# Hybrid attention and gating block on one core: one pool of 8 KB tiles to the end, the queries' norm factor in the sigmoids, output weights split in the first projection, last product's operands formed sooner

## The chip, the cores and the metric

One core of one Trainium2 chip. The metric is the device time of one execution in microseconds (us); less is better.

## The reference, cut to what matters

2048 rows of width 1024, all float32. An input projection feeds 8 heads of stick-breaking attention and a gated unit; an output projection, a residual and a squared-ReLU MLP (1024 to 4096 to 1024) follow.

```python
h = rmsnorm(x, norm_mix_g)
q, k, v, u, vg = split(h @ w_in)
z = q @ k.T / sqrt(64)                       # causal, per head
A[t,s] = sigmoid(z_ts) * prod_{s<j<t} (1 - sigmoid(z_tj))
a_out = A @ v
b_out = gelu(u) * (W_s @ layernorm(gelu(vg)) + b)
mix = concat(rmsnorm(a_out, g_a), rmsnorm(b_out, g_b))
x = x + mix @ w_out
act = square(relu(rmsnorm(x, norm_mlp_g) @ w_up))
out = rmsnorm(x + act @ w_down, norm_final_g)
```

## The kernel before, in words

**Products.** Every float32 operand is split in two parts (`split`, L81 to L85): ScalarE (ACT) rounds it to the high part, VectorE (DVE) subtracts that from the source for the low part. `mm3` (L89 to L91) then multiplies in three passes. A form of a 128x512 operand thus costs one ACT and one DVE instruction, and TensorE (PE) waits for both.

**Stages.** Rows go in four chunks c of 512. `proj([0, 1])` runs alone from the start; `transposed_cols` makes keys and queries (columns times rows): its products leave PSUM by a DVE product with the row factors `r_row` (L181) and a split of that. From about 230 us `attention` is a generator that `together` steps beside the matrix products: `weigh` (z from `kt` and `qt`, a sigmoid of -z to `kk` at L351 and one of z to `b` at L353, a running product `pr` on DVE, L356 to L360), `turn` (transposes L370, split to `aT`), `gather`. Where an output projection `Out(c)` needs heads that aren't done, the attention is stepped alone (`while steps[0] < ...: next(side)`). `Out.operands` loads the gated half from `b_d` (L473), the attention from `a_d`, and weights: for c = 0 `weights` reads `w_out` (L512), splits it with `outg_t` (L84, L85) and stores the parts to `wo_d` (L544); later chunks load those (L509).

**MLP.** Chunks 0 and 1: `up_plain`, `down_plain`. Chunks 2 and 3: seven products in place of eight (`up_seven` over 16 q, `down_seven` over 4 groups g, the order of products in `ORDER` and `ORDER_D`). `Rights` holds the seven right operands of `up_seven` as split pairs `hc` of 8 KB tiles; the first is formed ahead, the other six by `rest` at q = 0. `Lefts` and `operand` form the left ones per q. `keep_acts` (L582 to L586) forms three sums of the activations on DVE and stores all seven pieces to `s_d`; it stands at the end of each q, on DVE with the next operands behind it. `Down.load(0)` (L807) loads the first weights of the last product, called before the last evacuation of q = 15; `down_seven` then forms left operands (`raw` from `s_d`) and right ones (`right`, with three GpSimd (POOL) differences per half h, L846 to L848).

**Pools.** Up to the end of `down_plain` 8 KB tiles `t8` come from the pool `mp`. Then `mp` is closed and a pool `mlp` opened over the same memory, so a tile of `mlp` waits for everything that still reads what lay there, the stores of `down_plain`'s results to `out_y` among it. In the part quoted, `together(down)` finishes the plain product first:

```python
    rights = Rights(rm)
    ahead = Lefts(rm, 0)
    together(down)
    low.close()
    ...
        loads = Down(rm)
        together(up_seven(rights, rm, ahead, lambda: loads.load(0)))
```

The order of an engine's instructions is otherwise set by a scheduler that goes by the order of the code and the free buffers. SyncE (SP) issues most DMAs, in its own order.

Of the kernel before, what the change touches and what calls it, by code (L numbers as in the profile page):

```python
# [8 lines left out]
F32 = mybir.dt.float32  # L9
F32R = mybir.dt.float32r  # L10
# [24 lines left out]
def block_kernel(ctx: ExitStack, tc: tile.TileContext, x, x_t, gmix, w_in, ln_g, ln_b, sgw, sgb,  # L35
# [24 lines left out]


# [47 lines left out]
    def proj(cs, places, sp, gated_first, staging):  # L109
# [4 lines left out]
        def stage(shape):  # L114
            return staging[0].tile([P] + shape, F32, name=staging[1], bufs=staging[2])
# [29 lines left out]
        def norms(c, pl):  # L145
            for tb in range(NTB):
# [7 lines left out]
                r = sp.tile([P, 1], F32, name="x_r", bufs=3 * NTB)  # L154
                nc.gpsimd.tensor_tensor(r, m, mhalf[:, 0:1], ALU.pow)
                rs.append(r)
# [139 lines left out]
        yield from transposed_cols(1, k_d)  # L296
        yield from transposed_cols(0, q_d)
# [18 lines left out]
    def attention(cs):  # L316
# [4 lines left out]
        def weigh(u, tb):  # L321
# [25 lines left out]
            if diag:  # L347
                nc.tensor.matmul(z[:, L - P:L], ident_b, neg_b, start=False, stop=True)
            kk = kks[kk_n[0] % NKK]
# [112 lines left out]
    class Out:  # L462
# [40 lines left out]
        def weights(self, half, part):  # L503

            rm = self.rm
            w = rm.pair([4, 512])
            if self.c > 0:
                for i in range(2):
                    nc.sync.dma_start(w[i].bitcast(F32), wo_d[half, part, i])  # L509
                return w  # L510
            st = rm.t8([4, 512])
            nc.sync.dma_start(st, w_out[part * 512:(part + 1) * 512, half * 512:(half + 1) * 512]  # L512
                              .rearrange("(n p) d -> p n d", p=P))
            for n in range(4):
                split(w[0][:, n], w[1][:, n], st[:, n], outg_t[:, part * 4 + n:part * 4 + n + 1])
            return w

        def product(self):
# [9 lines left out]
            def group(half, part, m, rr):  # L528
# [13 lines left out]
                if c == 0:  # L542
                    for i in range(2):
                        nc.sync.dma_start(wo_d[half, part, i], ws[i].bitcast(F32))  # L544
# [34 lines left out]
    def keep_acts(q, acts):  # L579

        a11, a12, a21, a22, s1, s2, s4 = (acts[:, i] for i in (0, 1, 6, 3, 4, 5, 2))
# [33 lines left out]
    def down_plain(rm):  # L615
# [25 lines left out]
        for g in range(ND):  # L641
            lefts, rights = {}, {}
            for turn in range(4):
# [7 lines left out]
                if n not in rights:  # L651
                    rights[n] = right(n, g)
                a, b = lefts[c], rights[n]
# [21 lines left out]
    class Rights:  # L675
# [22 lines left out]
        def rest(self, step):  # L698
            if step == 0:
                self.keep(4, self.b11)  # L700
                self.keep(5, self.t2)
                self.keep(1, self.b21)
                self.minus(self.b21, self.b21, self.t2)
            elif step == 1:
                self.keep(6, self.b12)
            else:
                self.keep(3, self.b21)
                self.keep(2, self.b22)
# [21 lines left out]
    def up_seven(rights, rm, ahead, before_last):  # L730
        hc = rights.hc
        for q in range(16):
            l = ahead if q == 0 else Lefts(rm, q)
            s12, a11, a12, a21, a22, w0, w4 = l.s, l.a11, l.a12, l.a21, l.a22, l.w0, l.w4
            if q == 0:
                rights.rest(0)
# [13 lines left out]
            if q == 0:  # L750
                rights.rest(1)
# [3 lines left out]
            if q == 0:  # L755
                rights.rest(2)
            w2 = l.operand(a12)
            acts = rm.get("acts", [7, TC])
            c11, c21, c22, c12 = acts[:, 0, :], acts[:, 1, :], acts[:, 3, :], acts[:, 6, :]
            u2, u3 = rm.get("t2", [TC]), c22  # L760
# [29 lines left out]
            keep_acts(q, acts)  # L790
            yield

    class Down:


        def __init__(self, rm):
            self.rm = rm

        def load(self, g):

            self.bs = []
            for h in range(2):
# [7 lines left out]
                self.bs.append([v[0], v[2], v[1], v[3]])  # L810

    def down_seven(loads, rm):
# [19 lines left out]
        for g in range(NG):  # L832
            last_g = g == NG - 1
            if g > 0:
                loads.load(g)
            bs = loads.bs
            new = rm.get("acts", [2, 2, 512])

            def right(i, h):

                b11, b12, b21, b22 = bs[h]
                t2 = new[:, h]
                b = rm.w8([2, 2, 512])
                split(b[:, 0], b[:, 1], {0: b11, 5: t2, 1: b21, 6: b12, 4: b11, 3: b21, 2: b22}[i])
                if i == 0:
                    nc.gpsimd.tensor_tensor(b11, b12, b11, ALU.subtract)  # L846
                    nc.gpsimd.tensor_tensor(t2, b22, b11, ALU.subtract)
                    nc.gpsimd.tensor_tensor(b12, b22, b12, ALU.subtract)  # L848
                elif i == 1:
                    nc.gpsimd.tensor_tensor(b21, b21, t2, ALU.subtract)  # L850
                return b

            banks = {}
            for n, i in enumerate(ORDER_D):
                st = rm.raw8([4, TC])
                nc.sync.dma_start(st, s_d[g][i])
# [5 lines left out]
                tiles = []  # L862
# [192 lines left out]
```

## Time and profile before

| what | us |
|---|---|
| median of 3 runs (2518.34 to 2525.99) | 2518.61 |
| the profiled execution | 2518.97 |
| its span | 2517.2 |
| PE busy in the span | 2430.1 |
| DVE / ACT / POOL busy | 1694.0 / 1145.2 / 309.8 |

The span is the time from the first to the last instruction of the profiled execution; some 2 us lie around it. "Busy" counts matmuls by modelled ends, so a busy PE may run at half its clock: the granted clock is a column of its own (1.00 is 2.4 GHz, 0.5 is 1.2 GHz).

### The profile page before, as it was taken

What the parts mean: (1) busy time and instruction counts of PE and PEld (TensorE: products, weight loads), DVE (VectorE), ACT (ScalarE), POOL (GpSimd) and SP (SyncE); (2) the same over time, 40 slices, a digit from 0 to 9 for tenths busy, and PEclk for the clock granted to TensorE, in tenths of its full rate; (3) what the DMA queues carried; (4) which work ended last, traced back from release to release, by engine and by line L of the source; (5) the groups of instructions that cost most, each with busy time, mean ns of one, the idle gap of its engine ahead of it and who ended that gap; (6) DMA issues with size and microseconds to landing.
All of it is one profiled execution on the core that took longest, in us unless ns stands there. A gap on an engine that the chain in (4) does not pass through costs nothing.

```text
span 2517.2 us, 30341 instructions
## 1 busy us (share of the span) xinstructions
PE 2430.1 (97%) x11424; PEld 1991.5 (79%) x11424; DVE 1694.0 (67%) x2280; ACT 1145.2 (45%) x2004; POOL 309.8 (12%) x255
## 2 busy tenths in 40 slices
PE   8999999997899999999999899999989999999998
PEld 7887788876677888888877688888867888778886
DVE  4643678877767666666668878644667556677788
ACT  5422446445536555555555534322244444433333
POOL 1100011000000000000000000000113322314432
PEclk9999999997999999999989999999999999999999
DMA  9747977679544343433364533343523434753422
GB/s 378 265 141 240 333 260 243 214 211 330 173 164 150 121 126 120 123 115 117 126 255 162 181 130 117 112 182 134 216 85 137 156 141 153 281 218 120 167 101 101
DMA packets 158226, 446.59 MB, mean 177 GB/s; under 512 B 12544, under 2 KB 28928, under 8 KB 138624
## 3 DMA queue, kind: packets, MB, share of 16 engines
q1 hardware_dynamic: 149744, 417.39, 48.5%
q0 software_dynamic: 4032, 25.17, 2.4%
q10 hardware_dynamic: 4304, 2.10, 0.3%
q8 instruction: 90, 1.47, 0.2%
q14 instruction: 56, 0.46, 0.1%
HBM read 314.59 MB, written 130.02 MB: 177 GB/s over the span
## 4 chain that ended last, share of the span: by engine, by line
PE 86%; DVE 8%; issue 3%; DMA 3%; ACT 1%; POOL 0%; POOLq 0%; SPq 0%; DVEq 0%; ACTq 0%
PE mm L91 24%; PE mm L90 24%; PE mm L89 23%; PE tr L370 4%; PE av L389 2%; PE z L346 2%; PE av L388 2%; PE z L345 2%; DVE w L82 2%; DVE t L82 1%; DVE pr L359 1%; PE mm L498 1%; DVE aT L82 1%; PE mm L263 1%; DMA t<-b_d 1%
## 5 line engine op out<-in xcount | busy, mean ns | idle before, releaser
L89 PE MATMUL mm<-t,t 128*128 128x512 f32 x1280 | 503.5, 395 | 0.4 <-DVE t L82 0.4
L91 PE MATMUL mm<-t,t 128*128 128x512 f32 x1280 | 503.5, 393 | 0.0
L90 PE MATMUL mm<-t,t 128*128 128x512 f32 x1280 | 502.3, 393 | 0.0
L359 DVE TENSOR_TENSOR_SCAN pr<-kk,pr,zeros 128x513 f32<-128x513 f32 x192 | 246.3, 1284 | 119.5 <-ACT kk L351 119.0
L351 ACT ACTIVATE kk<-z 128x512 f32<-128x512 f32 (+2 forms) x320 | 172.3, 538 | 296.3 <-PE z L346 158.7
L89 PEld LDWEIGHTS mm<-t,t 128*128 128x128 f32 x1280 | 242.4, 189 | 51.2 <-DVE t L82 0.8
L91 PEld LDWEIGHTS mm<-t,t 128*128 128x128 f32 x1280 | 241.8, 189 | 52.0
L90 PEld LDWEIGHTS mm<-t,t 128*128 128x128 f32 x1280 | 242.1, 189 | 50.0
L81 ACT ACTIVATE aT<-tr 128x512 fp32r<-128x512 f32 (+1 forms) x320 | 173.7, 545 | 107.6 <-PE tr L370 105.9
L82 DVE TENSOR_TENSOR aT<-tr,aT 128x512 fp32r<-128x512 f32 (+1 forms) x320 | 191.1, 598 | 21.6 <-ACT aT L81 21.3
L370 PE MATMUL tr<-ident,b 128*128 128x128 f32 x1088 | 180.9, 279 | 21.9 <-DVE aT L82 17.8
L90 PE MATMUL mm<-w,w 128*128 128x512 f32 x448 | 176.4, 394 | 8.8 <-DVE w L82 8.6
L81 ACT ACTIVATE t<-t 128x1024 fp32r<-128x1024 f32 x104 | 104.7, 1060 | 172.7 <-DMA t<-in_w_down 110.8
L370 PEld LDWEIGHTS tr<-ident,b 128*128 128x128 f32 x1088 | 133.0, 143 | 58.4 <-DVE aT L82 26.6
L91 PE MATMUL mm<-w,w 128*128 128x512 f32 x448 | 175.6, 392 | 0.0
L353 ACT ACTIVATE b<-z 128x512 f32<-128x512 f32 (+2 forms) x320 | 172.1, 539 | 2.6 <-PE tr L370 2.6
L356 DVE TENSOR_TENSOR_SCAN pr<-kk,zeros 128x128 f32<-128x128 f32 (+3 forms) x128 | 104.5, 820 | 96.9 <-ACT kk L351 96.7
L81 ACT ACTIVATE w<-raw 128x512 fp32r<-128x512 f32 (+1 forms) x135 | 106.4, 801 | 132.3 <-PE mm L91 119.9
L91 PE MATMUL mm<-t,w 128*128 128x512 f32 x380 | 150.4, 396 | 2.8 <-DVE w L82 2.8
L82 DVE TENSOR_TENSOR w<-raw,w 128x512 fp32r<-128x512 f32 (+1 forms) x135 | 149.0, 1106 | 3.4 <-ACT w L81 2.9
L90 PE MATMUL mm<-t,w 128*128 128x512 f32 x380 | 149.1, 393 | 1.4 <-DVE t L82 1.4
L82 DVE TENSOR_TENSOR t<-t,t 128x1024 fp32r<-128x1024 f32 x104 | 123.6, 1225 | 39.1 <-ACT t L81 19.4
(214 smaller groups left out, 4765.5 us busy)
## 6 DMA issues: line engine op xcount, KB each, us to landing
w_in<-wi_d SPq DMA_DIRECT2D x40, 1024.0 KB, 8.4
kt<-k_d SPq DMA_DIRECT2D x160, 256.0 KB, 4.9
t<-in_w_down SPq DMA_DIRECT2D x28, 1024.0 KB, 5.1
s_d<-acts SPq DMA_DIRECT2D x16, 1792.0 KB, 6.2
raw<-s_d SPq DMA_DIRECT2D x28, 1024.0 KB, 4.8
t<-wo_d SPq DMA_DIRECT2D x24, 1024.0 KB, 6.9
wi_d<-w_in POOLq DMA_DIRECT2D x20, 1024.0 KB, 9.5
vt<-v_d SPq DMA_DIRECT2D x80, 256.0 KB, 2.7
```

The lines of the kernel that those rows point to most:

```text
L81: nc.scalar.activation(hi, src, AF.Copy)
L82: nc.vector.tensor_tensor(lo, src, hi.bitcast(F32), ALU.subtract)
L89: nc.tensor.matmul(ps, lh, rh, start=first, stop=False, skip_group_check=more)
L90: nc.tensor.matmul(ps, lh, rl, start=False, stop=False, skip_group_check=more)
L91: nc.tensor.matmul(ps, ll, rh, start=False, stop=last, skip_group_check=more)
L345: nc.tensor.matmul(z[:, :Z], ql, kt[:, 0, :Z], start=True, stop=False)
L346: nc.tensor.matmul(z[:, :Z], ql, kt[:, 1, :Z], start=False, stop=not diag)
L351: nc.scalar.activation(kk[:, :L], z[:, :L], AF.Sigmoid, scale=-QK_SCALE)
L353: nc.scalar.activation(b[:, :L], z[:, :L], AF.Sigmoid, scale=QK_SCALE)
L356: nc.vector.tensor_tensor_scan(pr[:, L - 1::-1], kk[:, L - 1::-1], zeros[:, :L], 1.0, ALU.mult, ALU.add)
L359: nc.vector.tensor_tensor_scan(pr[:, ::-1], kk[:, ::-1], zeros, carry[tb], ALU.mult, ALU.add)
L370: nc.tensor.transpose(tr[:, tb * P:(tb + 1) * P], bs[tb][:, j * P:(j + 1) * P], ident)
```

## The change

1. `mp` stays open to the end: `mlp` is gone, and with it the tiles `acts` and `t2`. The seven pieces of the activations lie in one 8 KB tile and two 4 KB ones, stored by three DMAs in place of one.
2. `Rights.rest` is a generator, stepped with the last two turns of `down_plain`.
3. `Down.first` loads and forms the operands of the last product's first step before the last evacuation of `up_seven`.
4. `w_out` is split in `proj([0, 1])` (`split_w_out`), stored to `wo_d` by POOL's queue; `Out.weights` only loads.
5. Queries are not multiplied by the row factor; the two sigmoids take it as a per-partition scale (`rq`), for which `norms` makes a negated copy on POOL.

```diff
@@ proj
+        def split_w_out():
+            for half in range(2):
+                for k in range(0, KD, 2):
+                    st, hi, lo = stage([2, 512]), stage([2, 512], F32R), stage([2, 512], F32R)
+                    nc.sync.dma_start(st, w_out[...])
+                    for n in range(2):
+                        split(hi[:, n], lo[:, n], st[:, n], outg_t[:, k + n:k + n + 1])
+                    for i, w in enumerate((hi, lo)):
+                        nc.gpsimd.dma_start(wo_d[half, k // 4, i, :, k % 4:k % 4 + 2, :], w.bitcast(F32))
+                    yield
...
+                nc.gpsimd.tensor_tensor(rq[:, 1, i:i + 1], r, mone, ALU.mult)
...
-                    t = sp.tile([P, TC], F32, name="gelu_t", bufs=3)
-                    nc.vector.tensor_tensor(t, ps, r_rows[ci], ALU.mult)
-                    split(st[:, 0, :], st[:, 1, :], t)
+                    if col == 0:
+                        split(st[:, 0, :], st[:, 1, :], ps, QK_SCALE)
...
+        if cs[0] == 0:
+            yield from split_w_out()
@@ attention
-            nc.scalar.activation(kk[:, :L], z[:, :L], AF.Sigmoid, scale=-QK_SCALE)
+            nc.scalar.activation(kk[:, :L], z[:, :L], AF.Sigmoid, scale=rq[:, 1, row:row + 1])
-            nc.scalar.activation(b[:, :L], z[:, :L], AF.Sigmoid, scale=QK_SCALE)
+            nc.scalar.activation(b[:, :L], z[:, :L], AF.Sigmoid, scale=rq[:, 0, row:row + 1])
@@ Out.product
-                if c == 0:
-                    for i in range(2):
-                        nc.sync.dma_start(wo_d[half, part, i], ws[i].bitcast(F32))
@@ keep_acts
-        nc.sync.dma_start(s_d[q // 4][:, :, q % 4, :].rearrange("i p t -> p i t"), acts)
+        nc.sync.dma_start(dst[0:4, :, q % 4, :].rearrange("i p t -> p i t"), acts)
+        nc.sync.dma_start(dst[4:6, :, q % 4, :].rearrange("i p t -> p i t"), s12)
+        nc.sync.dma_start(dst[6, :, q % 4, :], s4)
@@ Down
+        def first(self):
+            self.load(0)
+            self.made = self.make(0, ORDER_D[0])
@@ the end
-    together(down)
-    low.close()
+    while not placed:
+        next(down)
+    rest = rights.rest()
+    if together(down, rest, 0.5) is OPEN:
+        together(down)
+    for _ in rest:
+        pass
...
-        together(up_seven(rights, rm, ahead, lambda: loads.load(0)))
+        together(up_seven(rights, rm, ahead, loads.first))
```

The change has 35 lines more ahead of these functions, so its line numbers differ: L82, L663, L672, L692 and L582 to L585 of before are L86, L686, L695, L715 and L600 to L603 of the change.

**Order on DVE where `down_plain` ends.** The tiles `mm` are the plain product's banks, `t8` the kept right operands, `w8` their sources. Before:

```order
L663 TENSOR_TENSOR t8_12265<-mm_15921,t8_12265 128x512
L672 SCALAR_TENSOR_TENSOR t8_12265<-t8_12265,nf_r_15917,gfin_t_5092 128x1024
L73 TENSOR_SCALAR nf_m_15938<-nf_ssq_15936 128x1
L672 SCALAR_TENSOR_TENSOR t8_12265<-t8_12265,nf_r_15940,gfin_t_5092 128x1024
L82 TENSOR_TENSOR t8_15953<-w8_15032,t8_15952 128x1024 x2
L82 TENSOR_TENSOR t8_15959<-w8_15033,t8_15958 128x1024 x2
L82 TENSOR_TENSOR t8_15965<-w8_15035,t8_15964 128x1024 x2
L82 TENSOR_TENSOR w8_15973<-s12_15055,w8_15973 128x512
L692 TENSOR_TENSOR w8_15035<-w8_15035,w8_15033 128x1024
```

Now, the plain product's last evacuations (L686) and four of the six kept operands in turns:

```order
L86 TENSOR_TENSOR t8_15849<-w8_15044,t8_15848 128x1024
L686 TENSOR_TENSOR t8_12274<-mm_15807,t8_12274 128x512
...
L686 TENSOR_TENSOR t8_12276<-mm_15841,t8_12276 128x512
L86 TENSOR_TENSOR t8_15869<-w8_15046,t8_15868 128x1024 x2
L686 TENSOR_TENSOR t8_12276<-mm_15861,t8_12276 128x512
L715 TENSOR_TENSOR w8_15046<-w8_15046,w8_15044 128x1024
L86 TENSOR_TENSOR t8_15891<-w8_15045,t8_15890 128x1024 x2
L715 TENSOR_TENSOR w8_15046<-w8_15046,w8_15044 128x1024
L686 TENSOR_TENSOR t8_12274<-mm_15881,t8_12274 128x512
```

The kept operands stood behind the last result of the plain product; four of six now stand ahead of its last four evacuations.

**Order on DVE where `up_seven` ends.** `raw` is the left operand's source, `t` (or `acts`) the right one's. Before:

```order
L82 TENSOR_TENSOR w_18153<-t_18117,w_18153 128x1024
L82 TENSOR_TENSOR w_18159<-raw_18144,w_18159 128x1024
L782 TENSOR_TENSOR acts<-mm,t_18017 128x512
L82 TENSOR_TENSOR w_18162<-t_18121,w_18162 128x1024
L788 TENSOR_TENSOR acts<-mm,t_18017 128x512
L82 TENSOR_TENSOR w_18226<-raw_18220,w_18226 128x1024
L582 TENSOR_TENSOR acts<-acts 128x512
L583 TENSOR_TENSOR acts<-acts 128x512
L584 TENSOR_TENSOR acts<-acts 128x512
L585 TENSOR_TENSOR acts<-acts 128x512
L82 TENSOR_TENSOR w_18229<-acts,w_18229 128x1024
```

Now:

```order
L802 TENSOR_TENSOR t_18068<-mm,t_18069 128x512
L86 TENSOR_TENSOR w_18183<-t_18169,w_18183 128x1024
L808 TENSOR_TENSOR t_18068<-mm,t_18069 128x512
L86 TENSOR_TENSOR w_18189<-raw_18178,w_18189 128x1024
L600 TENSOR_TENSOR t_18201<-t_18068 128x512
L601 TENSOR_TENSOR t_18201<-t_18201,t_18068 128x512
L602 TENSOR_TENSOR t_18068<-t_18068 128x512
L603 TENSOR_TENSOR t_18069<-t_18068,t_18201 128x512
L86 TENSOR_TENSOR w_18192<-t_18173,w_18192 128x1024
L86 TENSOR_TENSOR w_18281<-raw_18279,w_18281 128x1024
```

The right operand of the second half of the first step (`w_18162` before, `w_18192` now) stood ahead of the four instructions of `keep_acts` and now stands behind them.

**Order on SP there and at the first output projection.** In the change, at the end of `up_seven`:

```order
L606 DMA s_d_103<-t_18035 128x2x512
L605 DMA s_d_103<-t_17931 128x4x512
L607 DMA s_d_103<-t_17932 128x512
L827 DMA t_18169<-in_w_down 128x4x512
L827 DMA t_18171<-in_w_down 128x4x512
```

The stores of q = 14 now go ahead of the first weights; before, three of the four weight loads went ahead of the one store. At `Out(0)`, before:

```order
L512 DMA t_5101<-in_w_out 128x4x512
L331 DMA vt<-v_d 128x512
L329 DMA kt<-k_d 64x2x512 x2
L334 DMA qt<-q_d 128x512
L331 DMA vt<-v_d 128x512
L473 DMA t_5111<-b_d 128x4x512
L475 DMA t_5113<-a_d 128x4x512
L400 DMA a_d<-ao 128x512
L544 DMA wo_d<-t_5099 128x2048
```

and now:

```order
L532 DMA t_5150<-wo_d 128x2048
L532 DMA t_5151<-wo_d 128x2048
L499 DMA t_5154<-b_d 128x4x512
L501 DMA t_5156<-a_d 128x4x512
L356 DMA vt<-v_d 128x512
L354 DMA kt<-k_d 64x2x512 x3
L359 DMA qt<-q_d 128x512
L356 DMA vt<-v_d 128x512
```

The load of the gated half from `b_d` stood behind the next heads' keys and queries and now stands ahead of them.

## Rows read from the trace of the kernel before

**Rows 1.** The page, part 1: busy time, share and instructions by engine.

```profile
PE 2430.1 (97%) x11424; PEld 1991.5 (79%) x11424; DVE 1694.0 (67%) x2280; ACT 1145.2 (45%) x2004; POOL 309.8 (12%) x255
```

**Rows 2.** Windows inside the two long stretches of attention beside matrix products.

```profile
core 0: us, PE busy (x) PEld busy (x) DVE busy (x) ACT busy (x) POOL busy (x), PEclk, DMA share, GB/s
270.00:540.00 270.00, 270.00 (x1399) 222.80 (x1399) 207.77 (x355) 137.90 (x298) 24.55 (x24) 1.00 0.78 257
800.00:1280.00 480.00, 480.00 (x2374) 395.67 (x2373) 308.37 (x396) 272.18 (x520) 9.95 (x13) 1.00 0.40 128
```

**Rows 3.** Windows (same columns) where PE stops, and one of the first projection.

```profile
63.00:126.00 63.00, 63.00 (x294) 52.54 (x294) 43.53 (x81) 29.00 (x44) 10.23 (x13) 1.00 0.70 264
...
550.00:580.00 30.00, 23.82 (x124) 17.61 (x123) 26.46 (x40) 18.97 (x41) 1.69 (x2) 0.99 0.70 186
580.00:610.00 30.00, 22.33 (x92) 18.31 (x93) 22.46 (x38) 21.44 (x42) 5.00 (x5) 0.61 0.92 332
...
1860.00:1900.00 40.00, 29.52 (x108) 22.48 (x107) 31.57 (x36) 22.78 (x33) 11.38 (x11) 0.87 0.28 105
2180.00:2215.00 35.00, 29.66 (x120) 23.90 (x119) 25.68 (x19) 14.43 (x18) 16.92 (x6) 0.90 1.00 388
2215.00:2240.00 25.00, 22.85 (x101) 18.61 (x100) 20.88 (x19) 8.21 (x9) 6.57 (x2) 1.00 0.33 126
```

**Rows 4.** Timeline of PE at the start of `up_seven`: start, duration, instruction, [idle before it].

```profile
1869.89 0.50 PE L89 MATMUL mm<-t,raw 128*128 128x512 f32 x1 [2.03 <-ACT t L81]
1874.56 0.79 PE L90 MATMUL mm<-t,raw 128*128 128x512 f32 x1 [4.17 <-DVE t L82]
...
1890.58 0.79 PE L91 MATMUL mm<-t,w 128*128 128x512 f32 x1 [2.48 <-DVE w L82]
```

**Rows 5.** Timeline of ACT there: splits of the kept operands.

```profile
1868.78 2.01 ACT L81 ACTIVATE t<-w 128x1024 fp32r<-128x1024 f32 x2 [1.68 <-DMA out_y<-t]
...
1873.24 3.90 ACT L81 ACTIVATE t<-w 128x1024 fp32r<-128x1024 f32 x4 [1.98 <-DMA out_y<-t]
```

**Rows 6.** Timeline of SP at the first output projection.

```profile
566.04 1.79 SPq L512 DMA_DIRECT2D t<-in_w_out  x1
...
575.33 0.43 SPq L473 DMA_DIRECT2D t<-b_d  x1
```

**Rows 7.** Timeline of ACT there.

```profile
579.00 2.56 ACT L84 ACTIVATE t<-t,outg_t 128x512 fp32r<-128x512 f32 x4 [2.75 <-DMA t<-in_w_out]
...
588.36 0.63 ACT L480 ACTIVATE t<-t 128x512 bf16<-128x512 f32 x1 [2.47 <-DMA t<-b_d]
```

**Rows 8.** Groups of DVE by line and form: total, mean ns, idle before.

```profile
L181 DVE TENSOR_TENSOR gelu_t<-mm,r_row 128x512 f32<-128x512 f32 x32 | 22.0, 689 | 49.4 <-PE mm L91 49.2
...
L85 DVE SCALAR_TENSOR_TENSOR t<-t,outg_t,t 128x512 fp32r<-128x512 f32 x16 | 11.0, 744 | 0.4 <-ACT t L84 0.4
```

**Rows 9.** Groups of ACT: the largest form of the sigmoid, and one with a per-partition scale.

```profile
L351 ACT ACTIVATE kk<-z 128x512 f32<-128x512 f32 x224 | 135.4, 605 | 192.3 <-PE z L346 158.7 <-PE z L348 30.7 <-DVE pr L359 2.0
...
L84 ACT ACTIVATE qkv_st<-mm,x_r 128x512 fp32r<-128x512 f32 x16 | 10.9, 685 | 23.0 <-PE mm L91 14.3 <-DMA v_d<-qkv_st 7.9 <-DMA q_d<-qkv_st 0.8
```

**Rows 10.** Timeline of PE where `down_seven` begins.

```profile
2188.69 0.39 PE L89 MATMUL mm<-w,w 128*128 128x512 f32 x1
...
2206.01 0.79 PE L90 MATMUL mm<-w,w 128*128 128x512 f32 x1 [5.34 <-DVE w L82]
```

**Rows 11.** Timeline of DVE there.

```profile
2174.93 0.69 DVE L582 TENSOR_TENSOR acts<-acts 128x512 f32<-128x512 f32 x1 [0.44 <-ACT acts L590]
...
2193.89 2.57 DVE L582 TENSOR_TENSOR acts<-acts 128x512 f32<-128x512 f32 x1 [0.23 <-ACT acts L590]
...
2204.74 1.21 DVE L82 TENSOR_TENSOR w<-acts,w 128x1024 fp32r<-128x1024 f32 x1
```

**Rows 12.** Timeline of POOL there.

```profile
2185.42 2.94 POOL L846 TENSOR_TENSOR t<-t,t 128x1024 f32<-128x1024 f32 x1 [21.22 <-DMA t<-in_w_down]
...
2195.88 2.86 POOL L846 TENSOR_TENSOR t<-t,t 128x1024 f32<-128x1024 f32 x1
```

**Rows 13.** DMA of 2176 to 2216 us: packets, bytes, mean rate.

```profile
DMA packets 5239, 15.04 MB, mean 376 GB/s; under 512 B 208, under 2 KB 208, under 8 KB 4470
```

More of the change, by code (lines that the diff above doesn't have):

```diff
@@ L59, in block_kernel @@
     sgb_t = const.tile([P, 8], F32, name="sgb_t")
+    rq = const.tile([P, 2, NC * NTB], F32, name="rq")
+    mone = const.tile([P, 1], F32, name="mone")
+    nc.gpsimd.memset(mone, -1.0)
     q_d = dram.tile([NH, 2, HD, T], F32, name="q_d")
@@ L503, in weights @@
         def weights(self, half, part):
-            rm = self.rm
-            w = rm.pair([4, 512])
-            if self.c > 0:
-                for i in range(2):
[L509 to L515, printed above, removed]
+            w = self.rm.pair([4, 512])
+            for i in range(2):
+                nc.sync.dma_start(w[i].bitcast(F32), wo_d[half, part, i])
             return w
@@ L576, in turn, with keep_acts @@
                     nc.sync.dma_start(h_d[self.c - 2][kk], self.hT[kk])
-    def keep_acts(q, acts):
-        a11, a12, a21, a22, s1, s2, s4 = (acts[:, i] for i in (0, 1, 6, 3, 4, 5, 2))
+    PLACE = (0, 1, 6, 3, 4, 5, 2)
+    def keep_acts(q, acts, s12, s4):
+        a11, a12, a21, a22 = (acts[:, i] for i in range(4))
+        s1, s2 = s12[:, 0], s12[:, 1]
         nc.vector.tensor_tensor(s1, a21, a22, ALU.add)
@@ L652, in down_plain @@
                     rights[n] = right(n, g)
+                if g == ND - 1 and turn == 2:
+                    placed.append(True)
                 a, b = lefts[c], rights[n]
@@ L696, in keep, with rest @@
             split4(t, src)
[L698 to L708, printed above, removed]
+        def rest(self):
+            self.keep(4, self.b11)
+            yield
+            self.keep(5, self.t2)
+            yield
+            self.keep(1, self.b21)
+            yield
+            self.minus(self.b21, self.b21, self.t2)
+            self.keep(6, self.b12)
+            yield
+            self.keep(3, self.b21)
+            yield
+            self.keep(2, self.b22)
     class Lefts:
@@ L754, in up_seven @@
             w3 = l.operand(a22)
-            if q == 0:
-                rights.rest(2)
             w2 = l.operand(a12)
-            acts = rm.get("acts", [7, TC])
-            c11, c21, c22, c12 = acts[:, 0, :], acts[:, 1, :], acts[:, 3, :], acts[:, 6, :]
-            u2, u3 = rm.get("t2", [TC]), c22
+            acts, both = rm.t8([4, TC]), rm.t4([2, TC])
+            c11, c21, c12, c22 = (acts[:, i, :] for i in range(4))
+            u2, u3 = both[:, 0, :], c22
             b1 = rm.ps()
@@ L789, in up_seven @@
             relu2(c12, c12)
-            keep_acts(q, acts)
+            keep_acts(q, acts, rm.t4([2, TC]), both[:, 1, :])
             yield
@@ L810, in load, with make, right @@
                 self.bs.append([v[0], v[2], v[1], v[3]])
+        def first(self):
+            self.load(0)
+            self.made = self.make(0, ORDER_D[0])
+        def make(self, g, i):
+            if self.made:
+                tiles, self.made = self.made, None
+                return tiles
+            rm = self.rm
+            if i == ORDER_D[0]:
+                if g > 0:
+                    self.load(g)
+                self.new = rm.t8([2, 2, 512])
+            st = rm.raw8([4, TC])
+            nc.sync.dma_start(st, s_d[g][PLACE[i]])
+            tiles = []
+            for h in range(2):
+                a = rm.w8([2, 2, TC])
+                split(a[:, 0], a[:, 1], st[:, 2 * h:2 * h + 2, :])
+                tiles.append((a, self.right(i, h)))
+            return tiles
+        def right(self, i, h):
+            b11, b12, b21, b22 = self.bs[h]
+            t2 = self.new[:, h]
+            b = self.rm.w8([2, 2, 512])
+            split(b[:, 0], b[:, 1], {0: b11, 5: t2, 1: b21, 6: b12, 4: b11, 3: b21, 2: b22}[i])
+            if i == 0:
+                nc.gpsimd.tensor_tensor(b11, b12, b11, ALU.subtract)
+                nc.gpsimd.tensor_tensor(t2, b22, b11, ALU.subtract)
+                nc.gpsimd.tensor_tensor(b12, b22, b12, ALU.subtract)
+            elif i == 1:
+                nc.gpsimd.tensor_tensor(b21, b21, t2, ALU.subtract)
+            return b
     def down_seven(loads, rm):
@@ L861, in down_seven @@
                 ps = banks[key]
-                tiles = []
-                for h in range(2):
-                    a = rm.w8([2, 2, TC])
-                    split(a[:, 0], a[:, 1], st[:, 2 * h:2 * h + 2, :])
-                    tiles.append((a, right(i, h)))
+                tiles = loads.make(g, i)
                 def passes(tb, k):
@@ L972, in block_kernel @@
         gfin_t = gains.tile([P, D], F32, name="gfin_t")
[L973 to L975 removed]
+        placed = []
+        mp = ctx.enter_context(tc.tile_pool(name="mp", bufs=1, reuse_waits="tile"))
+        rm = Room(mp, ps_mm, dict(t8=N8, t4=3))
+        gmlp_t = rm.t4([D])
         nc.sync.dma_start(gmlp_t, gmlp.broadcast_to([P, D]))
         nc.sync.dma_start(gfin_t, gfin.broadcast_to([P, D]))
[L978 removed]
         hTs = []
```

60 lines of the change are left out of this document (20 added, 40 removed).

## The prediction

> **What bounds the kernel now.** I read the page's busy times first: TensorE is busy for 2430.1 of 2517.2 us and the next engine, VectorE, for 1694.0 [rows 1]. So only two things can be won: time in which PE stands still, and time in which it runs at half clock after standing still. The windows tell where these are. In the long stretches PE is busy for the whole window at a granted clock of 1.00, with VectorE at 64% to 77% and ScalarE at 51% to 57% [rows 2]; removing work of those two engines there gives nothing. The idle time sits at seams between stages [rows 3], and the change touches three of them. Last I read the timelines of each seam for what PE waited for [rows 4 to 7, 10 to 12].
>
> A seam's loss is its idle PE time plus what the clock took: (1 - granted clock) x window, which is an upper end, since the clock is also low while PE stands still. Start of `up_seven`: 40 - 29.52 = 10.5 us idle and 0.13 x 40 = 5.2 us of clock, together 15.7. First output projection: 30 - 22.33 = 7.7 idle and up to 0.39 x 30 = 11.7 of clock after 580 us, and 6.2 idle before it; about 20 in all. Start of `down_seven`: 5.3 + 2.2 idle and 0.10 x 35 = 3.5 of clock, together 11.0. These three numbers are all that the parts below can win there.
>
> **Kept operands beside the plain product (part 2 of the change).** Now PE waits four times at the seam, first for ScalarE's splits and then for VectorE's [rows 4]. The splits begin late for a reason outside the engines: two groups of them wait for the landing of `out_y` stores [rows 5], since the new pool lies over the tiles that those stores read. Behind that come twelve splits one after another, at 1.0 us each on ScalarE (3.90 us for four [rows 5]). With one pool open to the end and the splits stepped with the last two turns, four of the six pairs stand ahead of the plain product's last evacuations, as the order on DVE shows. PE needs each product's operand only when the ones before it are through: a product is 48 passes, and in these rows a pass starts every 0.23 us, so a product is about 2.7 us; the two pairs still behind the seam come as the sixth and seventh of seven products, over 13 us after its start, and are six splits of about 1.1 us away. What can go wrong is ahead of the seam: splits between evacuations hold a PSUM bank by two splits and a subtraction, about 3.6 us against a product of 2.7 us, with three banks to go round. I leave 1.5 us of loss and take **-14**, with ends -9 (one bank wait of 3 us and the clock after it) and -15.5.
>
> **Output weights split in the first projection (part 4).** There the change adds 16 splits on each of ScalarE (2.56 us for four [rows 7]) and VectorE (744 ns [rows 8]), 10 and 12 us, and 12.6 MB of traffic. PE is busy for all of 63 us there, VectorE has 19.5 us free in that window and the DMA engines 30% of it [rows 3]: cost 0, ends -1 and +3 (the `w_in` loads of the query columns stand behind the new loads on SP, the `wi_d` stores behind the new ones on POOL's queue). If that cover went, the price would be the 12 us.
>
> What it takes away is at the first output projection. Attention is stepped alone there and VectorE is the limit: 26.5 and 22.5 of 30 us [rows 3]. Four splits stand in the middle of it, 2.56 us of ScalarE after 2.75 us idle for the weights' landing [rows 7], and 4 x 0.744 = 3.0 us of VectorE [rows 8]. Both go. The twelve others lie beside PE's work and give nothing. The order on SP moves too: the `b_d` load was issued 9 us after the weights, behind keys and queries of the next head [rows 6], and ScalarE and PE waited for it until 588.36 [rows 7]; now it stands ahead of these. It should land some 5 us sooner; the next head's keys and queries land later by the 2 MB and more that now go ahead, at 376 GB/s [rows 13] some 5 us. That head isn't the one drained, so I count 3.0 + 5 = **-8**; ends -2 (its late keys stop the attention instead) and -13 (two thirds of the 20).
>
> **Last product's first operands sooner (part 3).** PE goes straight from `up_seven` into the first step at 2188.69 and stops 12 us later for 5.34 us [rows 10]. Cause in the rows: the four instructions of `keep_acts` take 0.69 us each for q = 14 and 2.57 us and more for q = 15 [rows 11], from 2193.89 to 2204.74, while POOL works on its differences, 2.9 us each [rows 12]; each VectorE instruction ends about when a POOL one does. PE's next operand stands behind them. The change doesn't take this away: `keep_acts` stays on DVE, and the second half of the *first* step now stands behind it. Worse, the stores of q = 14, 1.84 MB, now go ahead of the first weights on SP: at 376 GB/s [rows 13] that is 4.9 us. POOL's first difference started when two weight tiles were there, at 2185.42 [rows 12]; now at 2190.3, and the first split of a tile, which lands 2.7 us sooner, ends about 2189.8: 1.1 us of idle PE. The half step then lasts 5.7 us to 2195.5. `keep_acts` meets three differences, 2190.3 to 2199, ends near 2200.2, and the waiting operand is ready at 2201.4: 5.9 us of idle, and 3.5 of clock as now. 1.1 + 5.9 + 3.5 = 10.5 against 11.0. I take **0**, ends -6 and +6 (the stores ending earlier or later, POOL meeting `keep_acts` or not).
>
> **Queries without the row factor (part 5).** Of the 32 products at L181, half go, 11.0 us of VectorE [rows 8], all in the projection where PE is the limit: 0. The 640 sigmoids get a per-partition scale. No row shows a sigmoid with one. The nearest is a 128x512 ScalarE copy out of PSUM with such a scale, 685 ns against 605 for the sigmoid [rows 9]: 80 ns each, 51 us of ScalarE in all. Ends: 0 and 80 ns. Where PE is busy throughout, ScalarE has 43% free and more [rows 2], so most of it is covered. It shows where attention runs alone and the chain sigmoid, running product, product sets the pace: about 100 sigmoids there x 80 ns = 8 us, some of it beside VectorE's own work: I take **+3**, ends 0 and +8.
>
> By "ScalarE: Activation LUTs", section "What ACT_TABLE_LOAD costs", of the Trainium skill each such operand adds about 93 ns; that would be an estimate of 60 us in place of 51, and speaks against this part.
>
> **Small things.** Sixteen POOL products of one column and 32 more store issues on SP have nobody waiting, except perhaps the first row factor at 239 us: 0, ends 0 and +2. Other seams (660 to 700, 1370 to 1410) may be reshuffled by the scheduler by a few us either way.
>
> **Sum.** -14 - 8 + 0 + 0 + 3 = -19, from the profiled execution's 2518.97: **2500 us**. That execution lies 0.4 us above the median, so nothing is to be corrected.
>
> **Rivals.**
> - *The sigmoids set the pace (slower).* If ScalarE with 80 ns more were the limit of a step of attention, all 51 us would come out: 2518.97 - 22 + 51 = 2548. It decides as soon as over 60% of the 51 is exposed (30 us, against 22 won and 7.6 of tolerance). Against it: PE busy for 100% of 750 us [rows 2]. For it: `kk` gates the running product. Chance 5%.
> - *The wait at the seam moves ahead of it.* Splits hold PSUM banks, or tiles still wait for `out_y`: of 14 us only 6 come, 2508. For it: three banks only, and the stores are as late as before [rows 5]. Chance 13%.
> - *The first output projection gains nothing*, since the next heads' keys are late: 2507 or 2508. Chance 14%.
> - *`down_seven` starts clean*: POOL's differences come after `keep_acts`, which take 0.69 us each again: 8 of the 11 us go, 2492. Chance 13%. For it: the differences start 4.9 us later than now. Against it: `keep_acts` starts later too, behind the same evacuation. The Trainium skill ("SBUF — State Buffer", section "Who interferes with whom") has VectorE with two SBUF inputs and GpSimd shut each other out for a whole instruction, whichever comes second; the 2.57 us in place of 0.69 agree, and by that rule one difference that runs into `keep_acts` is enough to hold all of it.
> - *The change doesn't do what it says*: the buffers of the one pool are handed out so that the kept operands wait as before, 2512 to 2516. Chance 5%.
>
> **How the numbers follow.** The forecast has the other 50%. The range takes in the clean start with the good ends of the other terms, 2488, and the seam or output rival with a bad end, 2513. One measurement of this kernel can tell 0.3%, 7.6 us, from no change: faster means below 2511. All of the forecast, nearly all of the clean start and most of the two middle rivals lie there: 0.86. Same 0.09, slower 0.05.
>
> **What would show it.** Start of `up_seven`: PE idle under 2 us and no half clock, or else waits on evacuations just ahead of it. First output projection: the wait for `b_d` gone or before 584, no L512. `down_seven`: a stop of about 6 us in the middle of the first step, in place of after it, with `keep_acts` still at 2.5 us and more. Sigmoids of 128x512 near 685 ns with PE still at 100% in the long windows. I am wrong if PE shows new idle time beside attention, or if the half clock stays at the seams.

## The result, and the profile after

The change takes 2499.6 us (median of 4 runs, 2497.61 to 2501.7) against 2519.45 before (median of 4, 2518.34 to 2525.99), a ratio of 0.9914 with a 95% interval of 0.9896 to 0.9931. The forecast was 2500. The profiled executions (2518.97 and 2500.81) are 18.2 us apart; the terms named below come to 21.2 us, and other stretches take 3.2 back. The sum was right, its terms not all: the two large gains came in the size that was forecast, the cost of the sigmoids did not show, and a gain of about 6 us and a loss of about 4 were not foreseen.

The windows of the changed kernel at the same seams (columns as in [rows 2]); `up_seven` begins 8 us and `down_seven` 18 us earlier than before:

```profile
226.00:260.00 34.00, 33.56 (x153) 27.01 (x152) 7.49 (x13) 8.64 (x17) 3.59 (x11) 1.00 0.98 300
550.00:580.00 30.00, 23.70 (x114) 17.70 (x113) 25.90 (x38) 18.96 (x39) 2.51 (x2) 0.89 0.76 254
580.00:610.00 30.00, 26.32 (x135) 22.02 (x134) 15.79 (x28) 14.02 (x28) 3.21 (x5) 0.89 1.04 345
1843.00:1883.00 40.00, 39.22 (x170) 31.47 (x169) 33.07 (x42) 22.74 (x37) 17.45 (x16) 1.00 0.41 145
2155.00:2190.00 35.00, 27.68 (x111) 21.45 (x110) 24.07 (x20) 11.45 (x16) 14.66 (x5) 0.90 1.03 361
2190.00:2215.00 25.00, 23.61 (x105) 19.25 (x104) 17.55 (x20) 10.06 (x10) 9.89 (x4) 1.00 0.39 156
```

The first of these windows before, which [rows 3] don't have:

```profile
226.00:260.00 34.00, 29.78 (x131) 23.38 (x130) 8.43 (x18) 9.94 (x21) 2.52 (x5) 0.95 0.83 259
```

PE was idle for 4.2 us there and is for 0.4 now. Against [rows 3]: the start of `up_seven` has 0.8 us of idle PE in place of 10.5, at full clock. After 580 us PE's clock is 0.89 in place of 0.61, and VectorE, which was the limit, has 15.8 us of work in place of 22.5. The start of `down_seven` is no better.

Windows cut the work at other places in each kernel. So I also took PE's records one by one: the time from a matmul to the next, less 0.227 us for a 128x512 pass (0.109 for 128x128 and so on), summed over the same stretch of PE's work. This is what PE loses there, to waits, clock and slow passes, in us (below zero where passes are quicker than 0.227 us), for the two kernels and five of the runs below:

| stretch of the work | before | change | undo_scale | undo_wout | late_splits | tied_keep_acts | tied_pad32 |
|---|---|---|---|---|---|---|---|
| first projection | 3.4 | 5.5 | 6.2 | 4.9 | 5.2 | 5.0 | 5.6 |
| next projection begins (225 to 260 us) | 6.8 | 1.1 | 8.6 | 0.4 | 1.2 | 0.4 | 0.6 |
| first output projection | 28.8 | 20.1 | 20.5 | 27.0 | 18.5 | 21.7 | 18.4 |
| start of `up_seven` | 15.8 | 1.5 | 0.5 | 1.5 | 9.9 | 1.5 | 1.2 |
| rest of `up_seven` | 2.4 | 6.0 | 6.0 | 6.0 | 5.9 | 6.0 | -0.4 |
| start of `down_seven` | 10.8 | 12.6 | 11.3 | 12.7 | 11.2 | 6.4 | 5.9 |
| whole program | 145.5 | 127.5 | 141.0 | 130.1 | 131.9 | 118.6 | 109.0 |

The other stretches differ by up to 4 us from run to run. So do some that stand here: at the first output projection late_splits, tied_keep_acts and tied_pad32 have the change's instructions in the change's order, and lose 18.4 to 21.7 us.

### The profile page after: what moved, and what is told of

Same layout as the page of the kernel before. It is cut to its first block, busy times and chain, and to the rows that moved or that the text cites. A ratio compares the mean times of both kernels' runs of the same rounds, so it can differ in the third digit from the quotient of the medians.

```text
span 2499.1 us, 30545 instructions
## 1 busy us (share of the span) xinstructions
PE 2427.0 (97%) x11424; PEld 1986.8 (79%) x11424; DVE 1686.5 (67%) x2264; ACT 1197.9 (48%) x2004; POOL 322.1 (13%) x288
## 4 chain that ended last, share of the span: by engine, by line
PE 83%; DVE 8%; DMA 4%; issue 3%; ACT 2%; POOL 0%; SPq 0%; DVEq 0%; POOLq 0%; ACTq 0%
PE mm L94 23%; PE mm L95 23%; PE mm L93 23%; PE tr L396 4%; PE av L414 2%; PE av L415 2%; PE z L370 2%; PE z L371 2%; DVE w L86 2%; DMA v_d<-qkv_st 1%; DVE pr L385 1%; DMA w_in<-wi_d 1%; PE mm L524 1%; DVE t L86 1%; DVE aT L86 1%
## 5 line engine op out<-in xcount | busy, mean ns | idle before, releaser
L377 ACT ACTIVATE kk<-z,rq 128x512 f32<-128x512 f32 (+2 forms) x320 | 201.7, 631 | 289.0 <-PE z L371 177.0
L86 DVE TENSOR_TENSOR aT<-tr,aT 128x512 fp32r<-128x512 f32 (+1 forms) x320 | 190.7, 599 | 25.3 <-ACT aT L85 25.2
L379 ACT ACTIVATE b<-z,rq 128x512 f32<-128x512 f32 (+2 forms) x320 | 201.0, 629 | 2.8 <-PE tr L396 2.7
L86 DVE TENSOR_TENSOR w<-raw,w 128x512 fp32r<-128x512 f32 (+1 forms) x135 | 149.9, 1112 | 0.9 <-ACT w L85 0.4
L95 PE MATMUL mm<-t,w 128*128 128x512 f32 x380 | 150.3, 396 | 0.0
L93 PE MATMUL mm<-t,w 128*128 128x512 f32 x380 | 150.2, 395 | 0.0
L94 PE MATMUL mm<-t,w 128*128 128x512 f32 x380 | 150.2, 395 | 0.0
```

The costliest lines, as they stand in the source:

```text
L86: nc.vector.tensor_tensor(lo, src, hi.bitcast(F32), ALU.subtract)
L93: nc.tensor.matmul(ps, lh, rh, start=first, stop=False, skip_group_check=more)
L94: nc.tensor.matmul(ps, lh, rl, start=False, stop=False, skip_group_check=more)
L95: nc.tensor.matmul(ps, ll, rh, start=False, stop=last, skip_group_check=more)
L379: nc.scalar.activation(b[:, :L], z[:, :L], AF.Sigmoid, scale=rq[:, 0, row:row + 1])
```

## The experiments

Each run changes the changed kernel, which stands at 2499.6 us, in one thing unless it says otherwise.

**Part 2 undone.**

```diff
-    rest = rights.rest()
-    if together(down, rest, 0.5) is OPEN:
-        together(down)
+    together(down)
...
+            if q == 0:
+                for _ in range(3):
+                    next(rest)
```

with the rest of `rest` stepped further on in q = 0 of `up_seven`, as before.

> The change with part 2 undone: the six kept operands are formed at q = 0 of up_seven again, the pool stays open to the end. Theory: the 14 us of the seam came from the place of the splits in the order, so about 2512 to 2514 us, with some 10 us of idle PE and half clock at the start of up_seven as before. Rival: they came from the one pool (no wait for stores of out_y), then at most 2504 us and an idle of under 4 us.

Measured 2498.59 us (5 runs, 2498.06 to 2500.08), ratio 0.9925 (0.9912 to 0.9938). PE's timeline there has one wait, as in the change:

```profile
1855.13 0.50 PE L93 MATMUL mm<-x,raw 128*128 128x512 f32 x1 [0.78 <-DVE t L686]
```

The reason is in the order: on all five engines the instructions stand exactly as in the change. Once the tiles come from the open pool, the scheduler puts the splits ahead by itself; where the code calls them has no effect. So this was a repeat of the change. The rival is right that the pool did it, for with part 4 or part 5 undone the seam loses no more either (1.5 and 0.5 us in the table). The run says nothing yet on what the pool did: the earlier place, or no wait for `out_y`.

**The splits forced behind the last evacuation**, the pool left open and part 2 undone as in undo_rest; `tie` holds the five sources of the kept operands:

```diff
+                    if g == ND - 1 and turn == 3 and tb == NTB - 1:
+                        for src in tie:
+                            nc.vector.scalar_tensor_tensor(src[:, 0, 0:1], y[:, 0:1], 0.0, src[:, 0, 0:1], ALU.mult, ALU.add)
```

> The change with one pool as it is, but the six kept operands tied by five one-column VectorE instructions to the last evacuation of the plain product, so that they are split behind it as before, with no store of out_y in their way. Theory: the gain at the seam comes from their earlier place, so some 5 to 10 us come back (2504 to 2510 us) with over 3 us of idle PE and half clock at the start of up_seven. Rival: the waits for out_y made the loss, then at most 2502 us and under 2 us of idle.

Measured 2506.14 us (2505.45 to 2509.3), ratio 0.9957 (0.994 to 0.9973): 6.5 us came back. The window:

```profile
1843.00:1883.00 40.00, 34.89 (x133) 26.24 (x132) 34.09 (x44) 22.44 (x33) 14.28 (x12) 0.91 0.25 88
```

5.1 us idle and the clock at 0.91. In the table the seam loses 9.9 us, against 1.5 with the splits ahead and 15.8 before. So of the 14 us some 8 are the place. The other 6 are argued: before, ScalarE's splits waited 1.68 and 1.98 us for stores of `out_y` [rows 5], but VectorE's half of them also stood behind the last result, a little later than here, and no run separates the two.

**Part 3 undone.**

```diff
-        together(up_seven(rights, rm, ahead, loads.first))
+        together(up_seven(rights, rm, ahead, lambda: loads.load(0)))
```

> The change with part 3 undone: only the weights are loaded ahead, the first operands are formed in down_seven. Theory: part 3 is worth nothing, so 2498 to 2502 us, and the stop of about 6 us moves from the middle of the first step to behind it. Rival: forming the operands early is worth the first half of the step, then 2504 us or more.

Measured 2502.44 us (2501.3 to 2504.39), ratio 0.9941 (0.9927 to 0.9954). PE's waits there:

```profile
2170.31 1.20 PE L93 MATMUL mm<-w,w 128*128 128x512 f32 x4 [1.22 <-ACT w L85]
2183.39 0.79 PE L94 MATMUL mm<-w,w 128*128 128x512 f32 x1 [6.07 <-DVE w L86]
...
2203.69 0.75 PE L94 MATMUL mm<-w,w 128*128 128x512 f32 x1 [2.15 <-DVE w L86]
```

The stop did not move behind the first step; it is as in the change. Neither theory fits: the early call does not set the order in the first step. What it does comes later: here four evacuations stand ahead of VectorE's next splits where the change has them behind, and PE's third wait is 2.15 us, with 3.4 us at half clock after it that the change doesn't have. That is worth some 2 to 3 us (15.0 us lost at the start of `down_seven` in place of 12.6).

**Part 4 undone**, with `Out.weights` and its stores as before.

```diff
-        if cs[0] == 0:
-            yield from split_w_out()
...
+            for n in range(4):
+                split(w[0][:, n], w[1][:, n], st[:, n], outg_t[:, part * 4 + n:part * 4 + n + 1])
```

> The change with part 4 undone: the output weights are split in the first output projection again. Theory: 8 us come back there, 2507 to 2509 us, with the time lost between 550 and 620 us as before. Rival: the gain there came from the order of the loads or from part 5, then 2498 to 2502 us.

Measured 2504.88 us (2503.52 to 2509.82), ratio 0.9954 (0.994 to 0.9969): 5.3 us come back, and 6.9 in the table. The windows:

```profile
550.00:580.00 30.00, 20.51 (x104) 15.06 (x103) 26.79 (x40) 20.83 (x43) 1.78 (x2) 0.88 0.82 223
580.00:610.00 30.00, 25.75 (x112) 21.53 (x112) 23.07 (x39) 21.07 (x38) 4.23 (x5) 0.72 0.91 341
```

VectorE is at 26.8 and 23.1 of 30 us again, as in [rows 3]. The theory holds for the size, at somewhat less than its 8. PE's longest wait there is another than before, though, for keys and not for `b_d`:

```profile
576.95 0.55 PE L355 MATMUL z<-kt,qt 128*128 128x256 f32 x1 [4.39 <-DMA kt<-k_d]
```

The first square on `b_d` is at 582.77 us and waits 0.35 us for the load. So the run does not confirm the 5 us that the prediction gave to the order of the `b_d` load.

**Part 5 undone.**

```diff
-                        split(st[:, 0, :], st[:, 1, :], ps, QK_SCALE)
+                    nc.vector.tensor_tensor(t, ps, r_rows[ci], ALU.mult)
+                    split(st[:, 0, :], st[:, 1, :], t)
...
-AF.Sigmoid, scale=rq[:, 1, row:row + 1])
+AF.Sigmoid, scale=-QK_SCALE)
```

> The change with part 5 undone: queries are multiplied by the row factor again and the sigmoids take a constant scale. Theory: the scale costs about 3 us where attention runs alone and gains nothing elsewhere, so 2496 to 2498 us, sigmoids of 128x512 at 605 ns. Rival: the shorter path of the queries took away the waits at 230 to 260 us, some 5 us, then 2501 to 2503 us and those waits are back.

Measured 2511.33 us (12 runs, 2505.74 to 2514.45), ratio 0.9973 (0.9963 to 0.9982). I expected a small gain and lost 12 us. PE's timeline after 240 us has the old waits again, first before:

```profile
240.28 0.49 PE L162 MATMUL mm<-ident,x_r 128*128 128x128 f32 x2 [1.49 <-POOL x_r L155]
...
254.89 0.39 PE L345 MATMUL z<-kt,qt 128*128 128x256 f32 x1 [2.73 <-DMA qt<-q_d]
```

then this run:

```profile
243.03 0.49 PE L180 MATMUL mm<-ident,rq 128*128 128x128 f32 x2 [1.49 <-POOL rq L173]
...
259.30 0.55 PE L365 MATMUL z<-kt,qt 128*128 128x256 f32 x1 [3.49 <-DMA qt<-q_d]
```

The rival had the place right: 7.5 us of the loss are there. The rest lies for the most part in three later stretches of PE's work, which stood at 610 to 620, 660 to 700 and 1500 to 1700 us before: each loses some 3 us more than in the change. The next run loses about as much in them without the loss at 240 us, so that part belongs to something else.

**Only the scale made constant**, in both sigmoids.

```diff
-AF.Sigmoid, scale=rq[:, 1, row:row + 1])
+AF.Sigmoid, scale=-1.0)
...
```

> The change with constant scales in the 640 sigmoids and nothing else altered; the queries' row factor is left out of the computation. This measures the cost of the per-partition scale alone. Theory: 3 us, so 2496 to 2498 us, sigmoids of 128x512 at 605 in place of some 685 ns. Rival: covered everywhere, 2498.5 to 2501 us; or more exposed than I counted, 2494 us or less.

Measured 2503.0 us (2500.17 to 2504.13), ratio 0.9937 (0.9924 to 0.9951). ScalarE's groups, first the change:

```profile
L377 ACT ACTIVATE kk<-z,rq 128x512 f32<-128x512 f32 x224 | 155.7, 696 | 203.4 <-PE z L371 177.0 <-PE z L373 24.0 <-DVE pr L385 1.5
L379 ACT ACTIVATE b<-z,rq 128x512 f32<-128x512 f32 x224 | 155.4, 695 | 2.8 <-PE tr L396 2.7
```

then this run:

```profile
L379 ACT ACTIVATE b<-z 128x512 f32<-128x512 f32 x224 | 135.6, 606 | 2.5 <-PE tr L396 2.5
L377 ACT ACTIVATE kk<-z 128x512 f32<-128x512 f32 x224 | 135.5, 605 | 180.3 <-PE z L371 152.7 <-PE z L373 25.3 <-DVE pr L385 1.3
```

Each of these sigmoids is 90 ns shorter, 448 of them 40 us, and the program isn't faster. But it is not a pure test: without `rq` as an operand the scheduler puts several hundred of PE's instructions elsewhere between 260 and 1500 us, and the order on VectorE and ScalarE changes too. Where the prediction put the cost, in PE's work that stood at 560 to 610 us before, this run loses 19.9 us and the change 19.4 by the count of the table. So no cost of the scale shows in these runs; that it is nothing is not shown.

**Part 5 undone as above, and the norms' squares out of the way.** The row norms write their squares to a scratch tile that only serves as a target; it is one of three `gelu_t` buffers, which the queries' products also take.

```diff
-                junk = sp.tile([P, D], BF16, name="gelu_t", bufs=3)
-                nc.scalar.activation(junk, xt, AF.Square, accum_out=ssq)
+                nc.scalar.activation(xt, xt, AF.Square, accum_out=ssq)
```

> Part 5 undone as in the run undo_scale, but the squares of the row norms are written over their source tile and no longer take one of the three gelu_t buffers, which the queries' products hold. Theory: what part 5 won at 230 to 260 us is the freed buffer, since the norms of the next chunk no longer wait for the queries' products; then the waits for row factors and queries there are gone (under 2 us lost in place of 8), and the time is 2498 to 2505 us against 2511 of undo_scale. Rival: it is the shorter path from the products to the queries' store; then the waits stay and the time too.

Measured 2498.38 us (2496.68 to 2501.25), ratio 0.9924 (0.9911 to 0.9937): as quick as the change, with all 16 products back. The window of 226 to 262 us, first of undo_scale:

```profile
226.00:262.00 36.00, 30.37 (x133) 23.94 (x131) 6.65 (x14) 7.90 (x17) 2.52 (x5) 0.95 0.77 228
```

and of this run:

```profile
226.00:262.00 36.00, 36.00 (x165) 29.45 (x163) 11.23 (x20) 8.21 (x17) 2.09 (x7) 1.00 0.97 309
```

PE has no idle time left. The first square of the next chunk starts at 222.40 us here, at 223.26 in the change and at 237.30 in undo_scale:

```profile
222.40 1.06 ACT L167 ACTIVATE st<-st 128x1024 f32<-128x1024 f32 x1 [2.00 <-DMA st<-in_x]
```

```profile
237.30 1.04 ACT L168 ACTIVATE gelu_t<-st 128x1024 bf16<-128x1024 f32 x1
```

So the gain of part 5 was neither VectorE's time nor the queries' path but a buffer.

**`keep_acts` of q = 15 later in the code**, behind the operands of the fourth step of `down_seven`.

```diff
+            if q == 15:
+                loads.late = lambda: keep_acts(...)
...
                 tiles = loads.make(g, i)
+                if g == 0 and n == 3:
+                    loads.late()
```

> The change with the four sums and three stores of keep_acts for q = 15 put behind the operands of the last product's fourth step. Theory: they, held by POOL's differences, make the stop of 6 us in the first step; without them ahead the stop and the half clock behind it go, 7 to 9 us: 2491 to 2493 us. Rival: the operand waits for its weights or for POOL as well, then it moves by under 3 us.

Measured 2498.56 us (2497.4 to 2500.72), ratio 0.9924 (0.9911 to 0.9936). A miss: the scheduler put the four sums where they were, and the stop was 6.09 us. So it says nothing on the theory, and I tied them:

```diff
+                loads.late = lambda b: (
+                    nc.vector.scalar_tensor_tensor(acts[:, 3, 0:1], b[:, 0, 0, 0:1].bitcast(F32), 0.0,
+                                                   acts[:, 3, 0:1], ALU.mult, ALU.add),
+                    keep_acts(q, acts, rm.t4([2, TC]), both[:, 1, :]))
...
+                if g == 0 and n == 2:
+                    loads.late(tiles[1][1])
```

> As late_keep_acts, but a one-column VectorE instruction makes the first sum of keep_acts for q = 15 wait for the second operand of the third step, since the place in the code alone did not move it. Theory: the sums, stretched by POOL's differences, make the stop of 6 us; now the second half's operand needs only its weights and ScalarE's split, 4 to 8 us go: 2491 to 2495 us, a stop under 2.5 us in the first step. Rival: POOL's differences hold VectorE's splits just as long, so the stop stays within 2 us of what it was or turns up one step later, 2496 us or more.

Measured 2493.05 us (2492.02 to 2496.46), ratio 0.9904 (0.9891 to 0.9917), 6.5 us less. PE's waits in the first steps:

```profile
2175.89 0.50 PE L94 MATMUL mm<-w,w 128*128 128x512 f32 x1 [1.82 <-DVE w L86]
2182.57 0.50 PE L94 MATMUL mm<-w,w 128*128 128x512 f32 x1 [0.95 <-DVE w L86]
2189.44 0.50 PE L94 MATMUL mm<-w,w 128*128 128x512 f32 x1 [1.13 <-DVE w L86]
```

One stop of 6 us became three short ones, with the clock at full speed. VectorE's splits there now take the POOL differences' pace (3.29 us in place of 1.2), so the contention is not gone, only what stood in its queue.

**The tiles 12 KB lower in the pool.** While the changed kernel has no wait in `up_seven`, it makes fewer passes per 100 us than before. Windows of before and of the change:

```profile
1905.00:2005.00 100.00, 100.00 (x438) 81.94 (x437) 62.92 (x88) 48.75 (x85) 30.50 (x22) 1.00 0.43 155
```

```profile
1890.00:1990.00 100.00, 100.00 (x432) 80.75 (x431) 60.77 (x81) 48.59 (x84) 29.75 (x22) 1.00 0.41 148
```

```diff
+        mp.tile([P, 4, 512], F32, name="t8", bufs=N8)
         gmlp_t = rm.t4([D])
```

> The change with the 8 KB tiles laid out at the start of the pool, ahead of the three 4 KB ones, 12 KB lower than in the change. In the change a pass of up_seven with a kept operand out of this pool takes 233.2 ns, before 229.2 ns; with the operand outside it 229 ns in both. Theory: the place of these tiles in memory makes the difference, so 229 to 230 ns again and some 4 us less, 2494 to 2496 us. Rival: it is what else goes on in up_seven (three stores, sums in the same pool), then 233 ns and 2498 to 2500 us.

Measured 2497.44 us (2495.72 to 2502.4), ratio 0.9921 (0.9908 to 0.9935), and the passes as slow as in the change (233.2 ns). The shift by 12 KB, a multiple of 512 bytes, is not it. But the two constants that part 5 adds also move all tiles of that side of SBUF, by 160 bytes (128 and 32). So two runs, on top of tied_keep_acts:

```diff
     mone = const.tile([P, 1], F32, name="mone")
+    const.tile([P, 8], F32, name="pad")
```

> The run tied_keep_acts with an unused constant of 32 bytes per partition behind mone. The change's two new constants moved every tile of the left side of SBUF up by 160 bytes: addresses that were 32 above a multiple of 64 bytes lie on one now, while the left operands of up_seven, on the right side, stay 32 above one. 32 bytes more bring both to the same remainder again. Theory: the remainder makes the slower passes, so 229 in place of 233 ns in up_seven and 3 to 5 us less than tied_keep_acts (2493.05): 2488 to 2490 us. Rival: addresses don't matter, 233 ns and 2492 to 2495 us.

Measured 2486.47 us (2482.18 to 2490.66), ratio 0.9883 (0.9866 to 0.9899).

> The same with 64 bytes: the left side's tiles lie on a multiple of 64 bytes (of 512 even) again, by another shift. Theory of the remainder: 233 ns as in the change and as in tied_keep_acts, 2492 to 2495 us. Rival, that any shift other than the change's is quick, or that 512 bytes are what counts: 229 ns or less and 2488 to 2490 us.

Measured 2493.89 us (2490.13 to 2495.23), ratio 0.9904 (0.989 to 0.9919). The windows in `up_seven`, first with 32 bytes:

```profile
1870.00:1970.00 100.00, 100.00 (x443) 82.81 (x442) 62.95 (x85) 49.65 (x87) 32.01 (x23) 1.00 0.42 148
```

then with 64:

```profile
1880.00:1980.00 100.00, 100.00 (x431) 80.50 (x430) 61.60 (x83) 48.85 (x85) 28.91 (x21) 1.00 0.41 151
```

443 passes against 431, with an unused 32 bytes, and 7.4 us between two programs whose instructions stand in one order. The theory of the remainder holds in its direction for these four layouts; with 32 bytes both the pass (226.7 ns) and the time are below what it gave. The run with 32 bytes is also the quickest version found: its median is 13 us below the change's, but the kernel before was also some 4 us quicker beside these two runs (2515.67 us), so against that the gain is about 9.

## Why the prediction was right, and where its steps were not

- **Start of `up_seven`, -14: right in size (15.8 to 1.5 us lost), wrong in cause.** The step "with one pool open to the end and the splits stepped with the last two turns" gave the stepping a share. It has none: undo_rest is the same program. The pool did all of it, some 8 us by the earlier place and the rest, as argued, by the waits for `out_y`. The bank waits that I left 1.5 us for came to one of 0.78 us. In the prediction "a product is 48 passes" is a slip: a product of `up_seven` has 12, and the 2.7 us that it goes on with is the time of 12.
- **First output projection, -8: right in size, its two parts not shown apart.** 28.8 to 20.1; undone alone it is 5 to 7 us. The wait for L512 is gone. The squares on `b_d` begin at 580.33 us in place of 588.36 [rows 7], of which some 2 us are the lead that the change has by 560 us; and undo_wout has the loss back with hardly a wait for `b_d`. What could be won there was more than the prediction's "about 20": its own three terms, 7.7, 11.7 and 6.2, make 25.6.
- **The new splits in the first projection, 0: right.** That stretch loses 5.5 us in place of 3.4, but 4.9 with part 4 undone, so at most about 0.6 us of it is theirs.
- **Start of `down_seven`, 0: nearly right, in its own steps.** PE's timeline in the change:

```profile
2171.08 1.21 PE L93 MATMUL mm<-w,w 128*128 128x512 f32 x4 [1.20 <-ACT w L85]
2184.16 0.80 PE L94 MATMUL mm<-w,w 128*128 128x512 f32 x1 [6.08 <-DVE w L86]
```

  1.1 and 5.9 us were forecast. VectorE shows `keep_acts` again at POOL's pace, as in [rows 11]:

```profile
2174.38 2.45 DVE L600 TENSOR_TENSOR t<-t 128x512 f32<-128x512 f32 x1 [0.37 <-ACT t L611]
2176.86 2.75 DVE L601 TENSOR_TENSOR t<-t,t 128x512 f32<-128x512 f32 x1
2179.54 2.83 DVE L602 TENSOR_TENSOR t<-t 128x512 f32<-128x512 f32 x1
2182.30 0.68 DVE L603 TENSOR_TENSOR t<-t,t 128x512 f32<-128x512 f32 x1
```

  POOL works on three differences from 2172.82 to 2181.82 us. Three sums are held, one by each; the fourth runs when POOL is idle and takes 0.68 us. So one difference holds one sum and not all of `keep_acts`, against what the prediction says under its rival. In all 12.6 against 10.8 us, +1.8. That `keep_acts` makes the stop, tied_keep_acts shows. That POOL sets their pace agrees with what the Trainium skill says in "SBUF — State Buffer", section "Who interferes with whom", on VectorE with two SBUF inputs.
- **Sigmoids, +3: not seen.** The price of one was right (685 forecast, 696 measured). By the Trainium skill, "ScalarE: Activation LUTs", section "What ACT_TABLE_LOAD costs", such an operand adds about 93 ns, and 91 over the 605 are measured. The step that failed is "about 100 sigmoids there x 80 ns = 8 us, some of it beside VectorE's own work": const_scale is not quicker, there or in all. That VectorE's work covers the whole cost is the likely reading and is not shown, since the order differs.
- **The removed products, 0: wrong, about -6.** "All in the projection where PE is the limit: 0" counted VectorE's time and not what the instruction's output tile held. The norms of the next chunk waited for a `gelu_t` buffer; 6.8 us of loss became 1.1.
- **Missing: the addresses, about +4 in `up_seven`.** Nothing in the prediction asks where tiles lie.

Sum of the terms as the profiles show them: -14.3 - 8.7 + 1.8 - 5.7 + 3.6 + 2.1 (first projection, where the forecast had 0) = -21.2, and +3.2 in other stretches, which also vary from run to run: -18.0. That the forecast of 2500 is met to the microsecond is luck: the gain of 5.7 that I had not seen and the 3 us for the sigmoids that did not show are made up by 3.6, 2.1 and 3.2 us of losses that I had not seen either.

## What to carry to other kernels

When a change removes an instruction, price the buffer its output held as well as its time: here the buffer was worth 6 us and the time nothing. Where a scheduler sets the order, the place of a call in the code may do nothing; what moves work is which buffers are free and what depends on what, so check that an edit, or its undoing, changes the order before reading its time. And after adding even a small constant tile, compare the passes per 100 us of a stage that is busy throughout: a change of pace there shows in no wait.

## What the runs showed that I had not expected

A pass of `up_seven` that reads a kept operand from this pool took 229.2 ns before, 233.2 in the change, 226.7 with 32 bytes more and 233.3 with 64 more (means over the stage). In the compiled programs these operands lie at addresses that are 288, 448, 480 and 0 above a multiple of 512 bytes, and the left operands at 480 in all of them: remainders of 32, 0, 32 and 0 by 64 bytes, against 32. Equal remainders went with the quicker passes. `down_plain` fits: both of its operands lie in this pool, so their remainders are equal in every layout, and its passes take 227 to 229 ns in all four.

The passes on the first kept operand fit only in part. Both of their operands lie at 480 on the other side of SBUF, and neither the change nor a pad moves them. Yet their mean is 229.5 ns before, 228.9 in the change, 226.7 with 32 bytes and 231.0 with 64: the last passes of each product take 226 to 227 in all four, the first ones up to 237 on average, and only with 32 bytes does none take more than 227. So the remainders of a pass's own two operands are not the whole account. What else counts, and why 480 is quicker than 288, stays open: it wasn't tried with other remainders, nor with the left operands moved.
